# A transformer block on one Trainium2 core: modulation sums turned a block sooner, dilated attention's steps four chunks later, the first gate's rows with priority, the background's modulation begun sooner

## The chip, the core and the metric

The kernel runs on one core of one Trainium2 chip. The metric is device time in microseconds (us). The kernel before took 1590.88 us, the median of three runs (1590.88, 1587.47, 1592.99). One further execution was recorded by the hardware profiler; every row quoted is from that one.

## The reference

One decoder block on x of 256 tokens by 2048 channels, in float32, with a conditioning vector c:

```python
mod = silu(c) @ w_ada + b_ada            # 2048 x 12288
shift1, scale1, gate1, shift2, scale2, gate2 = split(mod, 6)
h = rms_norm(x, norm1_gain) * (1 + scale1) + shift1
x = x + gate1 * mixing_sublayer(h, w_in, ...)
h = rms_norm(x, norm2_gain) * (1 + scale2) + shift2
x = x + gate2 * swiglu(h, w_ffn_in, w_ffn_out)
```

The mixing sublayer projects h by w_in into the columns of three mixers (stick-breaking attention, six heads; dilated window attention, six heads in three groups; gated linear attention, four heads) and into three sigmoid gates of 2048 columns each. Each mixer's output goes through its own matrix (w_br_sb, w_br_dil, w_br_gla), is multiplied by its gate, and the sum y goes through w_out. All weights are float32 and are read once.

## The kernel before, in words

**Products.** Every float32 operand is split in two parts, `hi` (rounded) and `lo` (the rest), and a product is three matmuls, hi·hi, hi·lo and lo·hi (L171 to L173 in `mm3`). The tokens are two tiles of 128, the channels of K are 16 chunks of 128, and a block is 512 columns of output: 6 matmuls of 128x128 by 128x512 for each chunk of K. Weights come two chunks at a time, 512 KB a DMA: SyncE issues the load into `raw`, ScalarE casts it to `whi` (L163; L522 in the grouped part), VectorE subtracts to `wlo` (L164; L523). Each has four buffers. One such weight group feeds 12 matmuls. ScalarE and VectorE work through their instructions in the order given, and so does SyncE's queue.

**Order.** The program is written in one order, and a scheduler that knows priorities lays it out on each engine. `prio()` moves what stands in it ahead, `issue_after` ties an instruction behind another one.

**The start: five groups of K.** h needs the modulation of its chunk, and that needs a pass over w_ada. So the first 16 blocks of w_in are computed group by group: GROUPS cuts the 16 chunks into 2, 3, 3, 3 and 5. While the blocks of group g run, `ada_stream` loads w_ada for group g + 1, and VectorE adds it up (`ada_mac`, L298: one multiply-add of 128 rows by the width). A finished piece is turned into columns by `turn_piece`: TensorE transposes it (L366), VectorE reduces (L368), adds the bias (L374) and finishes the scale (L377). `h_group` (L553 on) then makes H for the next group: ScalarE writes the high half (L487) and a float copy (L493), VectorE the low half (L494). The last block of a group is carried into the next one. The turning happens ahead of the group's last block (n == GROUPED - 1, L663), and h_group behind that block for the first and the fourth group change, ahead of it for the two between.

**The last group and the mixers.** The 16 blocks of the last group run with steps of the mixers put between their chunks of K (`steps` of `block`, tied behind the last matmul). `qk_norm` (L699) normalises the heads of q and k on ScalarE and VectorE (L717), `qk_turn` transposes them (L729) and ScalarE copies them back with the gain (L730). For dilated attention the turns are steps 7 and 10 of the block of columns 14·512, and the scores steps 13 and 15. Its weights and the mixture's rows follow with priority, then the gate blocks, the first with no steps, the second with the mixture's products.

**The background.** The rest of the modulation (shift2, gate1, scale2: 96 loads of 512 KB of w_ada) runs beside all this: `tick` in `block` advances a generator by the current rate for each weight group. A step issues one load on SyncE's queue (L413) and, where the ring of buffers is full, the multiply-add of an earlier one (L298). The ring has two tiles (AR0, AR1) until the blocks 13 to 15 of the last group, then four. The rate is 0 in blocks 0 to 4 of the last group, RATE_IN = 0.8 from block 5, RATE_MID = 0.7 from block 13 to the end of the y blocks. When gate1 is summed, `rows_of` (L1049) turns its four quarters of 512 columns into rows on all partitions: for each half quarter a cast (L1059), a subtraction (L1060) into `T6`, and, two ticks later, two matmuls with ones (L1064, L1065).

**The y blocks.** `y_block(n)` multiplies the three mixers' outputs by 512 columns of w_br_sb, w_br_dil and w_br_gla, and by the gates (L1213 to L1216). y(0) runs around 590 us, y(1) around 660 us.

Of the kernel before, what the change touches and what calls it, by code (L numbers as in the profile page):

```python
# [10 lines left out]
F32 = mybir.dt.float32  # L11
# [3 lines left out]
ALU = mybir.AluOpType  # L15
# [14 lines left out]
N_DIL = 6  # L30
N_GLA = 4
SEG_SHIFT1, SEG_SCALE1, SEG_GATE1, SEG_SHIFT2, SEG_SCALE2, SEG_GATE2 = range(6)
RATE_IN, RATE_MID = 0.8, 0.7

RATES_OP, RATES_FFN, RATE_OUT = (0.8, 0.3, 0.0), (0.75, 0.9, 0.7, 0.6), 0.5
GATE2_CUT = 12
# [4 lines left out]
GROUPED = 16  # L41
# [37 lines left out]
def trunk(ctx: ExitStack, tc: tile.TileContext, I, out):  # L79
    nc = tc.nc  # L80
# [24 lines left out]
    def acc_bank(shape=None):  # L105
        return psa.tile(shape or [P, NB], F32, tag="acc", name=nm("acc"))
# [4 lines left out]
    @contextmanager  # L111
    def prio(offset=AHEAD):

        with tc.high_priority(offset=offset):
            start = tc.cur_priority
            yield
            n = tc.cur_priority - start
        tc.cur_priority += n

    state = {"rate": 0.0}  # L120
# [387 lines left out]
    LAST = len(GROUPS) - 1  # L508
# [44 lines left out]
    def h_group(g):  # L553
        k0, k1 = GROUPS[g]
        sh, sc = gains[g]
        for k in range(k0, k1):
            make_h(k, sh[:, k - k0 : k - k0 + 1], sc[:, k - k0 : k - k0 + 1], g == 0)
# [96 lines left out]
    for g in range(LAST):  # L654
        base = ADA_BY[g - 1] if g else 0
        for n, b in enumerate(orders[g]):
            due = ADA_BY[0] * n // (GROUPED - 2) if g == 0 else base + (ADA_BY[g] - base) * (n + 1) // (GROUPED - 2)
            while done < min(due, ADA_BY[g]) and next(nxt, "end") != "end":
                done += 1
            if (g, n) == (0, 6):  # L660
                state.pop("casts_after", None)
                state.pop("macs_after", None)
            if n == GROUPED - 1:  # L663
                while turns and (g == LAST - 1 or turns[0][0] <= ADA_LATE + KC * (g + 1)):
                    turns.pop(0)[1]()
                if 0 < g < LAST - 1:
                    h_group(g + 1)
            if n % 2 == 0:
                two = early if (g, n) == (0, 0) else load_two(b - b % 2, *GROUPS[g])
            proj_block(g, b, two[b % 2], carry=n == GROUPED - 1)  # L670
        if g in (0, LAST - 1):
            h_group(g + 1)

    kc = S("KC", [P, 8, P])
    low_r, bias = S("T3", [P, P], F32R), kc[:, 1, :]
# [45 lines left out]
    def qk_turn(parts, behind=None):  # L721

        for b, h0, h1, gain in parts:
            for h in range(h0, h1, 2):
                ps = misc_bank([P, NT, 2, P])
                for t in range(NT):
                    for i in range(2):
                        with tc.issue_after(behind) if behind is not None else nullcontext():
                            nc.tensor.transpose(ps[:, t, i, :], heads(b)[:, t, h + i, :], ident)  # L729
                nc.scalar.activation(heads(b)[:, :, h : h + 2, :], ps, AF.Copy, scale=gain(h))  # L730
# [213 lines left out]
    dil_parts = ((4, 2, 4, dil_q), (5, 0, 4, dil_q), (6, 0, 4, dil_k), (7, 0, 2, dil_k))  # L944
# [44 lines left out]
    def mixture_rows(prob, sm, lse, den, spans):  # L989
        G = lambda x, g: x[:, :, 2 * g : 2 * g + 2]  # L990
        coef = const.tile([P, NT, N_DIL], F32, name="dcoef")
        for g in range(3):
            nc.vector.tensor_mul(G(coef, g), G(sm, g), den)
        nc.vector.reciprocal(coef, coef)
        nc.vector.tensor_mul(coef, coef, lse)
        for h in range(N_DIL):
            p = prob[h // 2][:, h % 2, :]
            for t, (a, b) in enumerate(spans):
                nc.vector.tensor_scalar(p[:, a:b], p[:, a:b], coef[:, t, h : h + 1], None, op0=ALU.mult)
# [49 lines left out]
    def rows_of(name, seg, acc):  # L1049

        quarters = [a[:, c : c + NB] for a in acc for c in (0, NB)]
        for _ in range(4):
            yield
        for q in quarters:
            ps = misc_bank([P, NB])
            for c in (slice(0, T), slice(T, NB)):
                hl = S("T6", [P, 2, T], F32R)
                hi, lo = hl[:, 0, :], hl[:, 1, :]
                nc.scalar.copy(hi, q[:, c])  # L1059
                nc.vector.tensor_tensor(lo, q[:, c], hi.bitcast(F32), op=ALU.subtract)  # L1060
                yield
                yield
                with tc.issue_after(state["mm"].ins):
                    nc.tensor.matmul(ps[:, c], ones_r, hi, start=True, stop=False)  # L1064
                    nc.tensor.matmul(ps[:, c], ones_r, lo, start=False, stop=True)  # L1065
            nc.scalar.copy(q, ps)
            yield
        state[name] = quarters
# [4 lines left out]
    def background():  # L1073
        for seg in (SEG_SHIFT2, SEG_GATE1, SEG_SCALE2):
            if seg == SEG_GATE1:
                acc = biased([S(f"T{4 + j}", [P, 2 * NB]) for j in range(2)], seg)
                yield from ada_segment_steps(acc, seg, rows_of("gate1", seg, acc), False)
            else:
                acc = S("ada", [P, D])
                yield from ada_segment_steps(halves(acc), seg, columns(seg, acc))  # L1080
        yield from last_macs()

    bg.append(background())
    for b in range(0, 3):
        proj_block(LAST, b)
    qk_norm(sb_parts)
# [13 lines left out]
    for b in range(13, GROUPED):  # L1100
        proj_block(LAST, b)

    dil_scores, dil_weights = dilated()
    dil_steps = {
        7: lambda: qk_turn(dil_parts[:2], state["mm"].ins),
        10: lambda: qk_turn(dil_parts[2:], state["mm"].ins),
        13: lambda: dil_scores(0, 3),
        15: lambda: dil_scores(3, 6),
    }
    pss = [acc_bank() for _ in range(NT)]  # L1110
    block(pss, h_at, w_in, 0, KC, 14 * NB, steps=dil_steps)
    rr = [A[13], S("A1", [P, NT, NB])]
# [8 lines left out]
    def gate_block(n, br, steps=None):  # L1121
        pss = [acc_bank() for _ in range(NT)]
        c0 = COL_G + br * D + n * NB
        block(pss, h_at, w_in, 0, KC, c0, steps=steps)
        g = S(gtags[n, br], [P, NT, NB])
        with prio():
            for t in range(NT):
                if n == 0:
                    state["gates0"] = nc.scalar.copy(g[:, t, :], pss[t])
                else:  # L1130
                    nc.scalar.activation(g[:, t, :], pss[t], AF.Sigmoid)
        gates[n, br] = g

    with prio():
        groups = dil_weights()
        mixture_rows(*groups)
    gate_block(0, 0)
    ring["tags"] = ("AR0", "AR1", "KC", "KD")
    od, turns = mixture(groups[0])
    gate_block(0, 1, turns)  # L1140
# [7 lines left out]
    for j in range(2):  # L1148
# [3 lines left out]
        for t in range(NT):  # L1152
            for h in (2 * j, 2 * j + 1):
                o, c = og[t][:, h, :], t * N_GLA + h
# [4 lines left out]
    for j in range(2):  # L1159
        hi = S(gtag[0][j], [P, 4, T], F32R)  # L1160
        lo = S(gtag[1][j], [P, 4, T], F32R)
        for t in range(NT):
            o = og[t].rearrange("p h d -> p (h d)")
            ps = misc_bank([P, 4, P])
            for i in range(4):
                c = 4 * j + i
# [346 lines left out]
    for i in range(NFF):  # L1513
# [32 lines left out]
        if ftags[2 * i] == ftags[2 * i + 1]:  # L1546
            hl = S(ftags[2 * i], [P, 2, 4, T], F32R)
            hi, lo = hl[:, 0], hl[:, 1]
# [99 lines left out]
    n, pss = 3, o[1]  # L1648
# [42 lines left out]
```

## Time and profile before

| | |
|---|---|
| runs | 1590.88, 1587.47, 1592.99 us |
| profiled execution | 1591.43 us |
| its span, first to last instruction | 1589.6 us |
| mean granted TensorE clock | 0.997 |
| TensorE busy | 1570.5 us, 99% |
| VectorE busy | 1335.3 us, 84% |
| ScalarE busy | 933.3 us, 59% |
| DMA | 402.25 MB, mean 253 GB/s |

Line numbers (L171) are those of the kernel's source. PE is TensorE, PEld its weight loads, DVE VectorE, ACT ScalarE, SP SyncE. Numbers at the end of buffer names are left out in rows of the profile. A row of the timeline gives the start and the length in us, and, in brackets, the idle time of the engine before it and what ended it. Matmuls overlap: one lasts 0.39 us in the rows, the next starts about 0.23 us behind it.

### The profile page before, as it was taken

The numbers are of one execution on the slowest core, as the hardware profiler recorded it, in microseconds if no ns is written. First come the engines' busy times: TensorE is split into PE (matmuls) and PEld (weight loads), VectorE is DVE, ScalarE is ACT, GpSimd is POOL, SyncE is SP. The second block draws the span as 40 slices with busy tenths as digits, with TensorE's granted clock in tenths as the row PEclk, the third lists the DMA queues.
The fourth block names the chain that finished last, engine by engine and source line by source line (L and its number), as shares of the span: only waits on it lengthen the run. The fifth ranks groups of instructions, "written<-read, shape, count | busy, mean of one in ns | idle before, by whom it ended". The sixth has DMA issues, their size and how long they took to land.

```text
span 1589.6 us, 20243 instructions
## 1 busy us (share of the span) xinstructions
PE 1570.5 (99%) x7190; PEld 1296.6 (82%) x7190; DVE 1335.3 (84%) x1615; ACT 933.3 (59%) x1331; POOL 13.3 (1%) x24
## 2 busy tenths in 40 slices
PE   8999999999999999999999999999999999999999
PEld 7788788888878878878888888888888888888887
DVE  6878886589888878878777887999999999999996
ACT  6777777887675534444445644555555555455553
POOL 1000000000000000000000000000000000000000
PEclk9999999999999999999999999999999999999999
DMA  9989987667787899988786786665565666975664
GB/s 339 331 309 311 317 313 278 207 210 233 225 275 261 287 330 331 309 290 310 239 280 233 271 290 217 202 198 197 200 210 196 202 199 205 311 236 193 218 213 147
DMA packets 185228, 402.25 MB, mean 253 GB/s; under 512 B 13278, under 2 KB 32388, under 8 KB 185128
## 3 DMA queue, kind: packets, MB, share of 16 engines
q1 hardware_dynamic: 183864, 397.75, 74.1%
q0 software_dynamic: 1088, 3.16, 0.6%
q8 instruction: 56, 0.92, 0.2%
q14 instruction: 44, 0.36, 0.1%
q10 hardware_dynamic: 176, 0.07, 0.0%
HBM read 395.68 MB, written 5.24 MB: 252 GB/s over the span
## 4 chain that ended last, share of the span: by engine, by line
PE 86%; DMA 4%; ACT 4%; DVE 4%; issue 2%; SPq 0%; ACTq 0%; DVEq 0%
PE acc L172 21%; PE acc L173 21%; PE acc L171 21%; PE misc L172 6%; PE misc L173 6%; PE misc L171 6%; DMA raw<-w_in 2%; ACT whi L163 1%; DVE wlo L164 1%; DMA raw<-w_br_gla 1%; PE misc L883 1%; PE misc L1198 0%; ACT A L549 0%; PE misc L467 0%; DVE wlo L523 0%
## 5 line engine op out<-in xcount | busy, mean ns | idle before, releaser
L171 PE MATMUL acc<-whi,H 128*128 128x512 f32 x1145 | 448.7, 393 | 3.6 <-ACT H L487 3.3
L172 PE MATMUL acc<-wlo,H 128*128 128x512 f32 x1145 | 448.6, 392 | 1.6 <-DVE wlo L523 1.6
L173 PE MATMUL acc<-whi,H 128*128 128x512 f32 x1145 | 446.9, 391 | 0.1
L163 ACT CAST whi<-raw 128x1024 fp32r<-128x1024 f32 (+1 forms) x232 | 237.0, 1023 | 246.2 <-PE acc L173 150.6
L164 DVE TENSOR_TENSOR wlo<-raw,whi 128x1024 fp32r<-128x1024 f32 (+1 forms) x232 | 274.0, 1185 | 111.0 <-ACT whi L163 104.8
L171 PEld LDWEIGHTS acc<-whi,H 128*128 128x128 f32 x1145 | 215.9, 189 | 48.7 <-ACT H L487 3.9
L172 PEld LDWEIGHTS acc<-wlo,H 128*128 128x128 f32 x1145 | 215.9, 189 | 47.9 <-DVE wlo L523 4.4
L173 PEld LDWEIGHTS acc<-whi,H 128*128 128x128 f32 x1145 | 215.5, 188 | 45.6 <-DVE H L494 0.6
L1420 ACT CAST whi<-raw 128x1024 fp32r<-128x1024 f32 (+1 forms) x163 | 155.3, 968 | 112.4 <-PE acc L173 42.3
L1406 DVE TENSOR_TENSOR wlo<-raw,whi 128x1024 fp32r<-128x1024 f32 (+1 forms) x163 | 178.1, 1115 | 10.8 <-ACT whi L1420 9.8
L523 DVE TENSOR_TENSOR wlo<-raw,whi 128x1024 fp32r<-128x1024 f32 x86 | 103.9, 1221 | 28.3 <-ACT whi L522 27.9
L549 ACT COPY A<-acc 128x512 f32<-128x512 f32 x129 | 73.5, 585 | 44.7 <-PE acc L173 43.3
L522 ACT CAST whi<-raw 128x1024 fp32r<-128x1024 f32 x86 | 89.7, 1053 | 7.5 <-DMA raw<-w_in 4.0
L173 PE MATMUL acc<-whi,A 128*128 128x512 f32 x234 | 91.1, 389 | 0.0
L172 PE MATMUL acc<-wlo,A 128*128 128x512 f32 x224 | 87.4, 390 | 0.8 <-DVE wlo L164 0.8
L171 PE MATMUL acc<-whi,A 128*128 128x512 f32 x224 | 87.6, 391 | 0.2 <-ACT whi L163 0.2
L171 PE MATMUL misc<-whi,H 128*128 128x512 f32 (+1 forms) x201 | 78.2, 389 | 0.0
L172 PE MATMUL misc<-wlo,H 128*128 128x512 f32 (+1 forms) x201 | 78.1, 388 | 0.0
L173 PE MATMUL misc<-whi,H 128*128 128x512 f32 (+1 forms) x201 | 77.9, 388 | 0.0
L1420 ACT CAST A<-raw 128x1024 fp32r<-128x1024 f32 (+1 forms) x47 | 45.9, 989 | 33.5 <-PE acc L173 12.8
L1406 DVE TENSOR_TENSOR A<-raw,A 128x1024 fp32r<-128x1024 f32 (+2 forms) x59 | 61.2, 1049 | 4.6 <-ACT A L1420 4.2
L539 ACT COPY acc<-A 128x512 f32<-128x512 f32 x97 | 56.1, 595 | 6.9 <-DVE A L551 6.0
(511 smaller groups left out, 2605.1 us busy)
## 6 DMA issues: line engine op xcount, KB each, us to landing
raw<-w_in SPq DMA_DIRECT2D x210, 512.0 KB, 5.1
raw<-w_ffn_in SPq DMA_DIRECT2D x176, 512.0 KB, 4.6
raw<-w_ffn_out SPq DMA_DIRECT2D x74, 512.0 KB, 5.4
AR<-w_ada SPq DMA_DIRECT2D x58, 512.0 KB, 5.0
raw<-w_out SPq DMA_DIRECT2D x32, 512.0 KB, 4.9
KC<-w_ada SPq DMA_DIRECT2D x23, 512.0 KB, 5.7
KD<-w_ada SPq DMA_DIRECT2D x20, 512.0 KB, 5.5
OS<-w_ada SPq DMA_DIRECT2D x24, 384.0 KB, 6.4
```

The costliest lines, as they stand in the source:

```text
L163: state["cast"] = nc.scalar.copy(hi[:, :n, :], raw[:, :n, :])
L164: state["split"] = nc.vector.tensor_tensor(lo[:, :n, :], raw[:, :n, :], hi[:, :n, :].bitcast(F32), op=ALU.subtract)
L171: nc.tensor.matmul(ps, lh, rh, start=start, stop=False, skip_group_check=seeded)
L172: nc.tensor.matmul(ps, lh, rl, start=False, stop=False, skip_group_check=seeded)
L173: state["mm"] = nc.tensor.matmul(ps, ll, rh, start=False, stop=stop, skip_group_check=seeded)
L522: nc.scalar.copy(hi, raw)
L523: nc.vector.tensor_tensor(lo, raw, hi.bitcast(F32), op=ALU.subtract)
L539: nc.scalar.copy(pss[t], A[b][:, t, :])
L549: nc.scalar.copy(A[b][:, t, :], pss[t])
L883: nc.tensor.matmul(ps[:n, t * N_GLA + h, :].rearrange("p (s l) -> p s l", l=L), at(f, h, t)[:, :n], odd(at(f, h, t)), start=True, stop=True,)
L1406: done = nc.vector.tensor_tensor(dst, x, y, op=ALU.subtract)
L1420: nc.scalar.copy(hi[:, :n, :], src)
```

## The change

Five edits. (1) The turning of the modulation's sums, and h_group, move one block up: the turning stands ahead of block 14 of each group, h_group ahead of block 15, for every group alike. (2) The cast and the subtraction of gate1's rows get priority. (3) The dilated turns go from steps 7 and 10 of their block to 11 and 14. (4) The scores go from that block's steps 13 and 15 into steps 1 and 3 of the first gate block, and the weights and the mixture's rows behind them into the same step 3. (5) The background begins at rate 0.5 in blocks 0 to 4 of the last group, and RATE_MID falls from 0.7 to 0.62.

```diff
-RATE_IN, RATE_MID = 0.8, 0.7
+RATE_FIRST, RATE_IN, RATE_MID = 0.5, 0.8, 0.62
...
-            if n == GROUPED - 1:
+            if n == GROUPED - 2:
                 while turns and (g == LAST - 1 or turns[0][0] <= ADA_LATE + KC * (g + 1)):
                     turns.pop(0)[1]()
-                if 0 < g < LAST - 1:
-                    h_group(g + 1)
+            if n == GROUPED - 1:
+                h_group(g + 1)
             if n % 2 == 0:
                 two = early if (g, n) == (0, 0) else load_two(b - b % 2, *GROUPS[g])
             proj_block(g, b, two[b % 2], carry=n == GROUPED - 1)
-        if g in (0, LAST - 1):
-            h_group(g + 1)
...
-                nc.scalar.copy(hi, q[:, c])
-                nc.vector.tensor_tensor(lo, q[:, c], hi.bitcast(F32), op=ALU.subtract)
+                with prio():
+                    nc.scalar.copy(hi, q[:, c])
+                    nc.vector.tensor_tensor(lo, q[:, c], hi.bitcast(F32), op=ALU.subtract)
...
     bg.append(background())
+    state["rate"] = RATE_FIRST
...
     dil_steps = {
-        7: lambda: qk_turn(dil_parts[:2], state["mm"].ins),
-        10: lambda: qk_turn(dil_parts[2:], state["mm"].ins),
-        13: lambda: dil_scores(0, 3),
-        15: lambda: dil_scores(3, 6),
+        11: lambda: qk_turn(dil_parts[:2], state["mm"].ins),
+        14: lambda: qk_turn(dil_parts[2:], state["mm"].ins),
     }
+    groups = []
+
+    def dil_last():
+        dil_scores(3, 6)
+        groups.extend(dil_weights())
+        mixture_rows(*groups)
+
...
-    with prio():
-        groups = dil_weights()
-        mixture_rows(*groups)
-    gate_block(0, 0)
+    gate_block(0, 0, {1: lambda: dil_scores(0, 3), 3: dil_last})
```

**Where VectorE's instructions stand at the first group change.** `tiny` are the sums, `mod1` the columns, `AR0` the sum of the group after next, `H4` the low half of h. Before:

```order
L523 TENSOR_TENSOR wlo_163_704<-raw_161_701,whi_162_703 128x1024
L296 TENSOR_SCALAR AR0_179_771<-OS2_180_772,csil_91 128x768
L523 TENSOR_TENSOR wlo_166_710<-raw_164_707,whi_165_709 128x1024
L523 TENSOR_TENSOR wlo_183_778<-raw_181_775,whi_182_777 128x1024
L368 TENSOR_REDUCE tiny_170_730<-misc_171_731 128x3
L368 TENSOR_REDUCE tiny_172_737<-misc_173_738 128x3
L374 TENSOR_TENSOR mod1_101<-tiny_170_730,bada_100 128x3
L523 TENSOR_TENSOR wlo_186_784<-raw_184_781,whi_185_783 128x1024
L374 TENSOR_TENSOR mod1_101<-tiny_172_737,bada_100 128x3
L523 TENSOR_TENSOR wlo_189_790<-raw_187_787,whi_188_789 128x1024
L377 SCALAR_TENSOR_TENSOR mod1_101<-mod1_101,vec_99 128x3
```

The same place with the change:

```order
L523 TENSOR_TENSOR wlo_167_719<-raw_165_716,whi_166_718 128x1024
L368 TENSOR_REDUCE tiny_161_701<-misc_162_702 128x3
L368 TENSOR_REDUCE tiny_163_708<-misc_164_709 128x3
L374 TENSOR_TENSOR mod1_101<-tiny_161_701,bada_100 128x3
L523 TENSOR_TENSOR wlo_170_725<-raw_168_722,whi_169_724 128x1024
L374 TENSOR_TENSOR mod1_101<-tiny_163_708,bada_100 128x3
L296 TENSOR_SCALAR AR0_179_771<-OS2_180_772,csil_91 128x768
L377 SCALAR_TENSOR_TENSOR mod1_101<-mod1_101,vec_99 128x3
L523 TENSOR_TENSOR wlo_183_778<-raw_181_775,whi_182_777 128x1024
L523 TENSOR_TENSOR wlo_186_784<-raw_184_781,whi_185_783 128x1024
L298 SCALAR_TENSOR_TENSOR AR0_179_771<-OD_191_814,csil_91,AR0_179_771 128x768
L523 TENSOR_TENSOR wlo_189_790<-raw_187_787,whi_188_789 128x1024
```

The columns (L377) now stand ahead of the splits wlo_183, wlo_186 and wlo_189. On TensorE the six transposes go from behind block 14's last matmul to ahead of its first.

ScalarE's order there is the same before and after but for buffer numbers; with the change:

```order
L522 CAST whi_182_777<-raw_181_775 128x1024
L549 COPY A14_173_742<-acc_171_728 128x512
L549 COPY A14_173_742<-acc_172_729 128x512
L522 CAST whi_185_783<-raw_184_781 128x1024
L539 COPY acc_194_821<-A14_173_742 128x512
L522 CAST whi_188_789<-raw_187_787 128x1024
L487 ACTIVATE H0_15_112<-T0_6_102,mod1_101 128x256
```

H (L487) did not move against the copies of block 14 and the casts.

**Where VectorE's subtraction of gate1's rows stands**, at the half of the rows that is the fifth of eight. `T6` is the half's low part, `ada` the sum of scale2. Before:

```order
L164 TENSOR_TENSOR wlo_1345_6180<-raw_1343_6177,whi_1344_6179 128x1024
L1215 TENSOR_TENSOR A8_1181_5427<-A8_1181_5427,acc_1314_6067 128x512
L1215 TENSOR_TENSOR A8_1181_5427<-A8_1181_5427,acc_1315_6068 128x512
L1216 TENSOR_TENSOR T3_1291_5966<-T3_1291_5966,A8_1181_5427 128x512 x2
L164 TENSOR_TENSOR wlo_1348_6186<-raw_1346_6183,whi_1347_6185 128x1024
L298 SCALAR_TENSOR_TENSOR ada_1246_5658<-KC_1312_6044,csil_91,ada_1246_5658 128x1024
L164 TENSOR_TENSOR wlo_1351_6192<-raw_1349_6189,whi_1350_6191 128x1024
L1060 TENSOR_TENSOR T6_1332_6142<-T5_1015_4533,T6_1332_6142 128x256
```

With the change (the line is L1059 there):

```order
L164 TENSOR_TENSOR wlo_1325_6087<-raw_1323_6084,whi_1324_6086 128x1024
L164 TENSOR_TENSOR wlo_1328_6093<-raw_1326_6090,whi_1327_6092 128x1024
L1059 TENSOR_TENSOR T6_1332_6130<-T5_967_4245,T6_1332_6130 128x256
L298 SCALAR_TENSOR_TENSOR ada_1218_5554<-AR1_1306_5995,csil_91,ada_1218_5554 128x1024
L164 TENSOR_TENSOR wlo_1339_6168<-raw_1337_6165,whi_1338_6167 128x1024
```

It stands five splits earlier: wlo_1339, 1342, 1345, 1348 and 1351 now follow it. On TensorE, before, two full weight groups (those of 1345 and 1348) come between the matmuls of this half and the first that reads wlo_1351; with the change the matmuls of the half stand behind the first group of 1339.

**SyncE's queue at the first y block.** Before, from the first load of w_br_gla to the second:

```order
L149 DMA raw_1203_5521<-w_br_gla 128x2x512
L413 DMA KC_1179_5398<-w_ada 128x1024
L413 DMA KD_1180_5413<-w_ada 128x1024
L413 DMA AR0_1194_5464<-w_ada 128x1024
L413 DMA AR1_1195_5479<-w_ada 128x1024
L149 DMA raw_1206_5527<-w_br_gla 128x2x512
```

With the change:

```order
L149 DMA raw_1206_5530<-w_br_gla 128x2x512
L413 DMA KC_1183_5422<-w_ada 128x1024
L413 DMA KD_1197_5473<-w_ada 128x1024
L413 DMA AR0_1203_5510<-w_ada 128x1024
L149 DMA raw_1209_5536<-w_br_gla 128x2x512
```

One background load less stands among the block's weights.

## The prediction

> **What bounds the kernel now.** I read the head of the profile first.
>
> ```profile
> span 1589.6 us, 20243 instructions
> ## 1 busy us (share of the span) xinstructions
> PE 1570.5 (99%) x7190; PEld 1296.6 (82%) x7190; DVE 1335.3 (84%) x1615; ACT 933.3 (59%) x1331; POOL 13.3 (1%) x24
> ```
>
> From the 40 slices of the span I take what the DMAs moved.
>
> ```profile
> GB/s 339 331 309 311 317 313 278 207 210 233 225 275 261 287 330 331 309 290 310 239 280 233 271 290 217 202 198 197 200 210 196 202 199 205 311 236 193 218 213 147
> ```
>
> TensorE is busy 99% of the span, so no gain larger than its idle time, plus whatever its slow clock costs, can come from a change that leaves every matmul in place. The profiled execution took 1591.43 us, 1.83 us more than its span and 0.55 us more than the median shown, 1590.88. The sum below is made against 1591.43, and 0.55 is taken off at the end. The slices of 330 and 331 GB/s are the stretch 556 to 636 us, to which I return.
>
> Next, the waits of TensorE: engine, line, what it waited for, then us in total, times, longest.
>
> ```profile
> PE acc L171 <- ACT H L487: 3.3, 2, 3.0
> PE misc L1065 <- DVE T L1060: 2.9, 1, 2.9
> PE misc L225 <- DMA H<-c: 2.4, 1, 2.4
> PE acc L172 <- DVE wlo L523: 1.6, 2, 1.0
> PE misc L729 <- DVE A L717: 1.4, 1, 1.4
> ```
>
> The rest of the list is 1.3 us or less each. The first, second and fifth row name lines that the change touches: the group's h (L487), the rows of gate1 (L1060), the dilated step's normalisation (L717). Of the small ones, one is weights that came late where the background's loads compete with them; it is quoted below.
>
> A stall costs more than its own length if the clock falls. The table by stretch shows for each: us, busy time of TensorE, its weight loads, VectorE, ScalarE and GpSimd, the granted clock, DMA share and GB/s. I laid the stretches on the edges at which the clock changed.
>
> ```profile
> 72.70:76.13 3.43, 0.59 (x3) 0.49 (x4) 3.23 (x6) 2.06 (x4) 0.00 (x0) 1.00 0.94 329
> 76.13:79.54 3.41, 3.41 (x10) 2.64 (x9) 3.27 (x6) 2.75 (x5) 0.00 (x0) 0.50 0.94 311
> 79.54:82.95 3.41, 3.41 (x16) 2.81 (x15) 1.61 (x2) 1.12 (x3) 0.00 (x0) 1.00 1.00 372
> ```
>
> The same about the second stall:
>
> ```profile
> 676.88:680.29 3.41, 0.56 (x6) 0.32 (x3) 1.92 (x4) 2.44 (x3) 0.00 (x0) 1.00 0.99 359
> 680.29:683.70 3.41, 3.39 (x9) 2.71 (x10) 2.63 (x4) 1.02 (x3) 0.00 (x0) 0.50 0.86 273
> ```
>
> Each of the two long stalls leaves a stretch of 3.4 us with TensorE busy for only 0.6 us, and the next stretch runs at clock 0.50: 10 and 9 matmuls begin in it instead of 16. At 3.41/16 = 0.213 us apiece that is 1.3 us and 1.5 us lost. The two stalls thus cost 3.0 + 1.3 = 4.3 us and 2.9 + 1.5 = 4.4 us.
>
> **First part: modulation sums one block sooner (L663 on).** This is the first stall, between group 0 and group 1.
>
> Its rows of TensorE (start and length in us, engine, line, operation, and in brackets the idle time before it), then ScalarE's, then VectorE's:
>
> ```profile
> 70.30 0.81 PE L366 MATMUL misc<-ident,ada 128*128 128x128 f32 x6
> 70.87 0.47 PE L171 MATMUL acc<-whi,H 128*128 128x512 f32 x1
> ...
> 75.54 0.50 PE L171 MATMUL acc<-whi,H 128*128 128x512 f32 x1 [3.04 <-ACT H L487]
> ```
>
> ```profile
> 72.47 1.05 ACT L522 CAST whi<-raw 128x1024 fp32r<-128x1024 f32 x1
> 74.89 0.60 ACT L487 ACTIVATE H<-T,mod 128x256 fp32r<-128x256 f32 x1 [1.37 <-DVE mod L377]
> ```
>
> ```profile
> 74.70 0.15 DVE L377 SCALAR_TENSOR_TENSOR mod<-mod,vec 128x3 f32<-128x3 f32 x1
> ...
> 76.75 0.42 DVE L494 TENSOR_TENSOR H<-scr,H 128x256 fp32r<-128x256 f32 x1
> ```
>
> TensorE runs out of work at 75.54 − 3.04 = 72.50, and waits for H until 75.54. H waited for the last modulation column on VectorE (74.70 + 0.15 = 74.85), although ScalarE was free from 72.47 + 1.05 = 73.52 on. The change turns the sums before block 14 instead of after it, so the six transposes go some 18 matmuls, 18 × 0.226 = 4 us, earlier (40.00 us for the 177 matmuls of the row of 278 below), and the order on VectorE puts L377 ahead of two weight splits of 1.2 us that stood before it. The columns are then ready well before 73.5. What is late next is ScalarE: its order is unchanged, and two copies of block 14, a cast, a copy and another cast stand ahead of H. The transposes now run ahead of block 14, so its end moves back by about the 0.57 us that they took (70.30 to 70.87) less one matmul of 0.23 that now comes after: some 0.35 us. ScalarE is free at 73.52 + 0.35 = 73.87, and H follows it: TensorE starts 0.65 us after H starts, as before (74.89 to 75.54), at 74.5 instead of 75.54. The stall shrinks from 3.04 to about 2.0 us: −1.05. It does not vanish.
>
> The second half of the product needs the low half (L494), which ran at 76.75. In the new order it stands behind one split less on VectorE, and follows at about 76.4. From 74.5 TensorE has 8 matmuls of 0.23 us that need only H, until 76.3: 0.1 to 0.5 us of new wait, I take 0.3.
>
> Does the clock still fall? With a stall of 2.0 us that stretch is busy for about 1.6 of 3.4 us. No row shows such a share. The nearest row is at the dilated step:
>
> ```profile
> 458.42:461.83 3.41, 2.04 (x11) 1.38 (x10) 2.07 (x3) 2.22 (x3) 0.00 (x0) 1.00 1.06 405
> 461.83:465.24 3.41, 3.41 (x24) 2.81 (x23) 3.37 (x6) 2.94 (x5) 0.00 (x0) 1.00 0.89 340
> ```
>
> There 2.04 us busy left the next stretch at 1.00; 0.59 us did not. 1.6 lies nearer 2.04, so I take no loss: −1.3, with 0 as the other end. First part: −1.05 − 1.3 + 0.3 = **−2.0 us**, between +0.3 (TensorE no sooner, and the low half late) and −4.3.
>
> The Trainium skill ("TensorE: Matmul & The Clock Gate", Part 1) puts the half rate behind at least one idle window of about 3.4 us, on a free-running grid. The grid agrees with the rows; the idle window does not quite, since a window with 0.59 us busy was already enough. By the page's rule neither 3.04 nor 2.0 us within a window would cost anything beyond itself, and this part would be worth −0.75 us in place of −2.0; the row at 76.13 speaks for the second.
>
> At the later group changes h is made earlier too. TensorE has no such wait there (of the 3.3 us of the first row of waits, 3.0 is this stall), so I count nothing.
>
> **Second part: priority for the rows of gate1 (L1059, L1060).**
>
> ScalarE's row, VectorE's two, and TensorE's:
>
> ```profile
> 677.62 1.04 ACT L163 CAST whi<-raw 128x1024 fp32r<-128x1024 f32 x1 [5.46 <-DMA raw<-w_in]
> ```
>
> ```profile
> 678.70 1.23 DVE L164 TENSOR_TENSOR wlo<-raw,whi 128x1024 fp32r<-128x1024 f32 x1 [1.49 <-ACT whi L163]
> 679.84 0.42 DVE L1060 TENSOR_TENSOR T<-T,T 128x256 fp32r<-128x256 f32 x1
> ```
>
> ```profile
> 680.31 0.58 PE L1065 MATMUL misc<-T,ones_r 128*128 128x256 f32 x1 [2.88 <-DVE T L1060]
> ```
>
> The subtraction of 0.42 us stood on VectorE behind a weight split that waited for a cast, and that for a DMA. TensorE stood behind it though the weights of that DMA were not its next ones. With priority the subtraction stands ahead of this split, behind splits of weights that TensorE needs sooner than the gate's rows in any case. What is late next: the split that it overtakes ended at 678.70 + 1.23 = 679.93, and its weights come two weight groups, 2 × 12 matmuls × 0.226 = 5.4 us, after the gate's rows. From 677.4, where TensorE would go on, that is 682.8: 2.9 us in hand. That cover hides it. All eight halves of the gate's rows are ordered this way; the other seven did not wait before. So the wait and the slow stretch go: −2.9 − 1.5 = **−4.4 us**, between 0 (the wait moves to weights that come late, below) and −4.4.
>
> **Third part: the dilated steps four chunks later (L1104 on).**
>
> VectorE's rows and TensorE's:
>
> ```profile
> 459.76 1.22 DVE L164 TENSOR_TENSOR wlo<-raw,whi 128x1024 fp32r<-128x1024 f32 x1 [1.61 <-ACT whi L163]
> 460.90 2.49 DVE L717 TENSOR_TENSOR A<-A,tiny 128x512 f32<-128x512 f32 x4
> ```
>
> ```profile
> 461.64 1.04 PE L729 MATMUL misc<-ident,A 128*128 128x128 f32 x6 [1.38 <-DVE A L717]
> ```
>
> The normalisation of A5 stood on VectorE behind a split whose weights were late, and the transposes (L729) waited. In the program the steps go four chunks later; in TensorE's order they stand within the same weight group of the gate block as before, since the normalisation itself sets when they can run. On VectorE half of A5 now passes the split, the other half is still behind one, and two multiply-adds of the background, 1.28 us each by the row below, are new ahead of the whole chain.
>
> ```profile
> 453.47 1.28 DVE L298 SCALAR_TENSOR_TENSOR ada<-AR,csil,ada 128x1024 f32<-128x1024 f32 x1
> ```
>
> They may push the stall up by 2.6 us, or the split-free half may take away the 1.38. I take **0**, between −1.4 and +2.6. The scores and the mixture's rows move with the steps into the first gate block. Their consumer, the mixture's transposes at chunk 4 of the second gate block, stays 17 chunks of six matmuls, 17 × 6 × 0.226 = 23 us, behind: nothing. The 16 transposes of shift2's columns come earlier, between the same matmuls: nothing.
>
> **Fourth part: the background's rates.** RATE_FIRST starts the background in the last group's first five blocks.
>
> ```profile
> 278.00:318.00 40.00, 40.00 (x177) 32.81 (x176) 23.47 (x35) 35.85 (x97) 0.00 (x0) 1.00 0.67 206
> ```
>
> And the stretch of the y blocks:
>
> ```profile
> 598.00:638.00 40.00, 40.00 (x183) 33.22 (x182) 33.20 (x34) 18.99 (x22) 0.00 (x0) 1.00 0.93 332
> ```
>
> Five blocks of three weight groups (two chunks of K, 12 matmuls, 2.72 us) at 0.5 make 7.5 steps, each a DMA of 0.52 MB and 1.28 us on VectorE: 9.6 us on an engine busy for 23.5 of 40, and 3.9 MB in 40 us, 98 GB/s on top of 206. 304 GB/s is less than the 332 seen. Both hide it. RATE_MID from 0.7 to 0.62 takes 0.08 × 0.52 MB per weight group, 15 GB/s, off the stretch that runs at 332. There the weights of w_br_gla came late:
>
> ```profile
> 594.18 0.51 PE L171 MATMUL acc<-whi,A 128*128 128x512 f32 x1 [0.20 <-ACT whi L163]
> 595.45 0.50 PE L172 MATMUL acc<-wlo,A 128*128 128x512 f32 x1 [0.76 <-DVE wlo L164]
> ```
>
> In SyncE's order three background loads instead of four stand between the first and the second of these weights. One load less (0.52 MB at 332 GB/s, 1.6 us) covers 0.96 us of waits: **−1.0 us**, between 0 and −1.0. Against it I put **+0.5 us** for the weights of the next y block: seven background loads stand on SyncE's queue up to their last one, as before, but three of them now stand right ahead of the third, and no row there shows a wait now, and the price is between 0 and the 1.0 of its sister.
>
> **Sum.** −2.0 − 4.4 + 0 − 1.0 + 0.5 = −6.9 us: 1591.43 − 6.9 = 1584.5 on the profiled execution's basis, less 0.55: **1584.0 us**, −0.43%. If each part reaches its better end: −4.3 − 4.4 − 1.4 − 1.0 = −11.1, 1579.8.
>
> **Rivals.**
> (a) *The order of ScalarE decides, and the first part gives nothing.* H waits for casts whose DMAs also compete; the clock still falls. For it: five instructions stand ahead of H. Against: ScalarE idled 1.37 us before H. −4.4 − 1.0 + 0.5: 1590.88 − 4.9 = 1586.0. Here this part of the change does not do what it says.
> (b) *The DMA becomes the bound after 558 us.* TensorE comes 4.4 us earlier to every weight after 677, and if the queue had no slack, the wait returns at the next late weight: only the first part stays, 1590.88 − 2.0 = 1588.9. For it: 332 GB/s is the most any slice shows, and a cast waited 5.46 us for a DMA at 677. Against: the weights overtaken had 2.9 us in hand, and the stretch from 680 on already falls to 273 GB/s.
> (c) *The early background makes weights late in the last group.* Its loads stand on SyncE's one queue ahead of weights, each waits until VectorE has released one of only two buffers, and VectorE's multiply-add may itself stand behind a split. At the dilated step this mix cost 1.4 us, at the gate's rows 2.9 + 1.5 = 4.4. If three of the five blocks between 278 and 318 us pay 4.4 each, 13.2 − 6.9 = +6.3: 1597.2, slower. Two such stalls leave +1.9, no change that shows; it decides from the third on. Against: VectorE at 59% and 206 GB/s there.
>
> **How the numbers follow.** A measurement of this kernel can tell about 0.3%, 4.8 us, from no change: faster is below 1586.1, slower above 1595.7. Forecast 0.50, (a) 0.15, (b) 0.24, (c) 0.11. The forecast's own range is 1579.8 to 1586.1. (a) lies on the edge: two thirds of it count as faster. Faster 0.50 + 0.10 = 0.60, same 0.05 + 0.24 = 0.29, slower 0.11. The range takes in the forecast's best end, (a) and (b) with the 2.6 us of the dilated step on top (1588.9 + 2.6 = 1591.5), and leaves (c) out: 1579.5 to 1592.
>
> **What would show it.** Right: no wait at the gate's rows near 675 us and no stretch at clock 0.50 behind it; a wait of about 2 us for H near 74 us without a slow stretch; the wait for A5 near 460 us still there; none at w_br_gla near 590. Wrong: waits for weights (L171 or L172 on casts and splits) in the last group's blocks before 320 us, at the y blocks, or behind the gate's rows, or a new slow stretch anywhere.

## The result, and the profile after

With the change the kernel takes 1588.57 us, the median of 20 runs (1584.67 to 1593.55); before, 1591.27 us in 20 runs (1587.26 to 1594.34). The ratio is 0.9986, with a 95% interval of 0.9977 to 0.9995: faster, by 0.14%, some 2.2 us (2.7 us by the medians), where 0.43% was forecast. The forecast had called less than 0.3% no change; with twenty runs of each kernel the interval leaves 1 out. The profiled execution of the changed kernel took 1588.55 us.

The head of its profile:

```profile
span 1586.7 us, 20238 instructions
## 1 busy us (share of the span) xinstructions
PE 1566.8 (99%) x7190; PEld 1294.0 (82%) x7190; DVE 1334.0 (84%) x1615; ACT 932.2 (59%) x1331; POOL 12.5 (1%) x24
```

The span is 2.9 us shorter, and the work is the same: 7190 matmuls. The waits of TensorE, in the same columns as before, tell more:

```profile
PE misc L727 <- DVE A L715: 3.7, 3, 2.3
PE acc L172 <- DVE wlo L523: 3.6, 4, 1.5
PE misc L225 <- DMA H<-c: 2.4, 1, 2.4
PE acc L171 <- ACT H L487: 2.3, 2, 2.0
```

Against the list of before, the wait at the gate's rows (2.9 us) is gone, and the wait for H went from 3.3 to 2.3 us. But the splits L523 went from 1.6 to 3.6 us, and the normalisation (L715 now, L717 before) from 1.4 to 3.7. So 3.9 us less on two rows and 4.3 us more on two others, and what is left of the gain is mostly the two slow stretches of the clock, 1.3 + 1.5 us, which this execution doesn't have. The first of the two comes and goes from run to run, with the change and without it, as the last section shows; so this one pair of traces flatters the change.

**The first group change came out as forecast.** TensorE, then ScalarE, then VectorE:

```profile
74.08 0.50 PE L171 MATMUL acc<-whi,H 128*128 128x512 f32 x1 [2.03 <-ACT H L487]
...
76.71 0.73 PE L173 MATMUL acc<-whi,H 128*128 128x512 f32 x2 [0.52 <-DVE H L494]
```

```profile
72.48 1.05 ACT L522 CAST whi<-raw 128x1024 fp32r<-128x1024 f32 x1
73.43 0.61 ACT L487 ACTIVATE H<-T,mod 128x256 fp32r<-128x256 f32 x1
```

```profile
69.28 0.16 DVE L377 SCALAR_TENSOR_TENSOR mod<-mod,vec 128x3 f32<-128x3 f32 x1
...
76.24 0.42 DVE L494 TENSOR_TENSOR H<-scr,H 128x256 fp32r<-128x256 f32 x1
```

The columns are ready at 69.4 instead of 74.9. H follows directly on the cast, with no idle time before it: ScalarE's order has become the limit. The stall is 2.03 us (forecast 2.0), the new wait for the low half 0.52 (forecast 0.3). The stretch with the stall is busy for 1.94 us, and the next runs at full clock:

```profile
72.61:76.02 3.41, 1.94 (x8) 1.42 (x8) 3.41 (x4) 3.41 (x7) 0.00 (x0) 1.00 0.98 369
76.02:79.44 3.42, 2.90 (x13) 2.25 (x13) 3.38 (x6) 1.41 (x2) 0.00 (x0) 1.00 0.92 303
```

**The gate's rows too.** TensorE goes from the weights through the two matmuls with ones and on, with no idle time:

```profile
675.79 0.28 PE L1063 MATMUL misc<-T,ones_r 128*128 128x256 f32 x1
675.91 0.29 PE L1064 MATMUL misc<-T,ones_r 128*128 128x256 f32 x1
676.03 0.40 PE L171 MATMUL acc<-whi,H 128*128 128x512 f32 x1
```

**What came in their place, first: splits in the grouped part.** VectorE and TensorE around 192 us with the change:

```profile
191.19 0.89 DVE L298 SCALAR_TENSOR_TENSOR AR<-OS,csil,AR 128x640 f32<-128x640 f32 x1 [1.74 <-DMA OS<-w_ada]
192.43 0.89 DVE L298 SCALAR_TENSOR_TENSOR AR<-OD,csil,AR 128x640 f32<-128x640 f32 x1 [0.35 <-DMA OD<-w_ada]
193.23 2.36 DVE L523 TENSOR_TENSOR wlo<-raw,whi 128x1024 fp32r<-128x1024 f32 x2
```

```profile
194.50 0.50 PE L172 MATMUL acc<-wlo,H 128*128 128x512 f32 x1 [1.53 <-DVE wlo L523]
```

The two splits stand behind two multiply-adds, and VectorE waits for their loads. (The next waits of this row are 1.03 us at 212 us and 0.85 us at 247 us.) On SyncE's queue these loads were issued after two loads of weights:

```profile
183.56 2.03 SPq L519 DMA_DIRECT2D raw<-w_in  x2
185.63 0.43 SPq L337 DMA_DIRECT2D OS<-w_ada  x1
186.11 0.43 SPq L337 DMA_DIRECT2D OD<-w_ada  x1
```

Before, the load of OS was issued with two others ahead of those weights:

```profile
181.72 1.38 SPq L337 DMA_DIRECT2D OS<-w_ada  x3
185.87 2.03 SPq L519 DMA_DIRECT2D raw<-w_in  x2
187.94 0.43 SPq L337 DMA_DIRECT2D OD<-w_ada  x1
```

**Second: the stick-breaking turn.** VectorE's rows and TensorE's around 315 us with the change:

```profile
315.23 1.28 DVE L298 SCALAR_TENSOR_TENSOR ada<-AR,csil,ada 128x1024 f32<-128x1024 f32 x1
317.62 0.29 DVE L800 TENSOR_TENSOR T<-raw,T 128x128 fp32r<-128x128 f32 x1 [1.12 <-ACT T L799]
...
319.73 2.55 DVE L164 TENSOR_TENSOR wlo<-raw,whi 128x1024 fp32r<-128x1024 f32 x2 [0.57 <-PE acc L173]
322.20 1.29 DVE L715 TENSOR_TENSOR A<-A,tiny 128x512 f32<-128x512 f32 x2
```

```profile
322.94 0.77 PE L727 MATMUL misc<-ident,A 128*128 128x128 f32 x5 [2.31 <-DVE A L715]
```

Two of the early background's multiply-adds (the other at 313.94) and a subtraction that waited for a late load push the normalisation of A0 behind two more splits; TensorE waits 2.31 us.

### The profile page after: what moved, and what is told of

Its sections match the earlier page's. It is cut to its first block, busy times and chain, and to the rows that moved or that the text cites. A ratio compares the mean times of both kernels' runs of the same rounds, so it can differ in the third digit from the quotient of the medians.

```text
span 1586.7 us, 20238 instructions
## 1 busy us (share of the span) xinstructions
PE 1566.8 (99%) x7190; PEld 1294.0 (82%) x7190; DVE 1334.0 (84%) x1615; ACT 932.2 (59%) x1331; POOL 12.5 (1%) x24
## 3 DMA queue, kind: packets, MB, share of 16 engines
q1 hardware_dynamic: 183864, 397.75, 74.2%
## 4 chain that ended last, share of the span: by engine, by line
PE 82%; DMA 7%; DVE 5%; ACT 4%; issue 2%; SPq 0%; ACTq 0%; DVEq 0%
PE acc L173 19%; PE acc L172 19%; PE acc L171 19%; PE misc L172 6%; PE misc L173 6%; PE misc L171 6%; DMA T<-w_ada 2%; DMA raw<-w_in 2%; DMA OS<-w_ada 2%; DVE wlo L523 1%; ACT whi L163 1%; DMA A<-w_ada 1%; ACT scr L707 1%; PE misc L881 1%; DVE wlo L164 1%
## 5 line engine op out<-in xcount | busy, mean ns | idle before, releaser
L523 DVE TENSOR_TENSOR wlo<-raw,whi 128x1024 fp32r<-128x1024 f32 x86 | 104.1, 1221 | 25.8 <-ACT whi L522 25.6
```

Source lines behind the costliest of these rows:

```text
L523: nc.vector.tensor_tensor(lo, raw, hi.bitcast(F32), op=ALU.subtract)
```

## The experiments

Two theories stood against each other. **A:** the parts that were forecast gave what was forecast, and two side effects took most of it back: turning sooner reorders the loads of w_ada further on, and the early background makes the stick-breaking turn late. **B:** one shared cause, or VectorE's load in general, so that no single edit gives the time back. Ratios are to the kernel before, runs of which stood beside each.

**e1: no early background.**

```diff
-RATE_FIRST, RATE_IN, RATE_MID = 0.5, 0.8, 0.62
+RATE_FIRST, RATE_IN, RATE_MID = 0.0, 0.8, 0.62
```

> The changed kernel with rate 0 in blocks 0 to 4 of the last group, as before the change; all else changed. Theory A (the early background's multiply-adds and loads made the stick-breaking turn late): the wait of L727 for A L715 near 320 us falls from 2.3 us to under 0.5, and the time is some 2 us below the changed kernel's, ratio to before about 0.997. Theory B (that wait comes from the new modulation turns ahead of it): it stays near 2.3 us, ratio about 0.9985.

1585.92 us, ratio 0.9971 (0.9956 to 0.9985). The wait of L727 near 320 us is gone; what remains of that row, 0.5 us, lies at the dilated step. The splits stay late:

```profile
PE acc L172 <- DVE wlo L523: 3.5, 2, 1.9
...
PE misc L727 <- DVE A L715: 0.5, 1, 0.5
```

As A expected. The early background costs some 2.4 us by the ratios; their intervals overlap, and the pair e2 and e5 gives the same, 2.2 us.

**e2: old turns.** The turning and h_group as before, the rest changed:

```diff
-            if n == GROUPED - 2:
+            if n == GROUPED - 1:
                 while turns and (g == LAST - 1 or turns[0][0] <= ADA_LATE + KC * (g + 1)):
                     turns.pop(0)[1]()
-            if n == GROUPED - 1:
-                h_group(g + 1)
+                if 0 < g < LAST - 1:
+                    h_group(g + 1)
...
+        if g in (0, LAST - 1):
+            h_group(g + 1)
```

> The changed kernel with the modulation sums turned where they were before, all else changed. Theory A (turning sooner saves 2.1 us at the first group change and costs 3.0 us at later splits L523, since the loads of w_ada come later in SyncE's order): the 3.0 us wait for H near 75 us and its slow stretch are back, the waits for L523 splits fall from 3.6 us to about 1.6, net about 1 us faster than the changed kernel, ratio to before about 0.998. Theory B (the later splits were late for another cause): waits for L523 stay near 3.6 us and the time is 2 us above the changed kernel's, ratio about 1.000.

1585.61 us, ratio 0.9969 (0.9954 to 0.9984). The wait for H is back, the splits are in time:

```profile
PE acc L171 <- ACT H L487: 3.1, 1, 3.1
...
PE acc L172 <- DVE wlo L523: 0.2, 1, 0.2
```

The splits are as A expected, and the time by more: by the ratios 2.7 us below the changed kernel. The two intervals overlap, but e4 and the pair e1 and e5 show the same sign. So the edit that shortens the first stall is, as a whole, a loss. One thing that A expected did not come: behind the wait for H the clock stayed at 1.00 here. Another stall, of 1.43 us for the multiply-adds at 26 us, left two stretches at 0.50; the first of them:

```profile
23.11:26.53 3.42, 2.00 (x12) 1.41 (x10) 2.10 (x3) 0.48 (x1) 0.00 (x0) 1.00 1.03 382
26.53:29.94 3.41, 3.41 (x11) 2.63 (x11) 2.34 (x11) 2.33 (x5) 0.00 (x0) 0.50 1.02 386
```

(In this execution the wait of the stick-breaking turn was shorter, 1.3 us: the subtraction behind the late load began at 316.79 us, against 317.62 in the changed kernel.)

**e3: only the priority.** The kernel before, with `prio()` around the cast and the subtraction of gate1's rows.

> The kernel before with only the priority of the gate1 rows. Theory A (that wait and its slow stretch cost 4.4 us and nothing behind them takes the wait over): no wait at L1065, none new for weights behind 675 us, ratio 0.997. Theory B (the wait moves to weights that come late): waits on casts or splits of 2 to 4 us between 675 and 720 us, ratio 0.999 to 1.000.

1585.41 us, ratio 0.9971 (0.9958 to 0.9985): 4.6 us by the ratio (the interval allows 2.4 to 6.7). No wait at L1065 is left, and none above 0.3 us behind it, as A expected. This one edit gives twice what the whole change gives. (The profiled execution, 1583.56 us, was the fastest of the ten, and no stretch of it ran at a clock of 0.50.)

**e4: only the turns.** The kernel before, with the first edit alone.

> The kernel before with only the modulation sums turned one block sooner. Theory A: wait for H near 72 us about 2 us and no slow stretch behind it (2.1 us gained), L523 splits 3.6 us instead of 1.6 or more (3.0 us lost), ratio 1.0005. Theory B (the late splits belong to the other edits): L523 waits 1.6 us, ratio 0.9987.

1592.94 us, ratio 1.0022 (1.0007 to 1.0036). By itself the edit makes the kernel slower, by 3.5 us, which is more than A's 0.8. The wait for H is 2.0 us and the splits' 3.4, as A expected, but behind the first stall the clock fell, which A had excluded:

```profile
70.48:73.89 3.41, 1.44 (x7) 0.86 (x5) 1.92 (x2) 3.41 (x7) 0.00 (x0) 1.00 1.05 388
73.89:77.30 3.41, 3.35 (x8) 2.67 (x9) 3.41 (x5) 3.40 (x7) 0.00 (x0) 0.50 0.88 294
```

Two more slow stretches follow, behind a late split (from 248.0 us) and behind the wait at the gate's rows (from 688.3 us). Why the loss is more than 0.8 us is not settled. The profiled execution was the slowest of the twelve, 1598.60 us, and has waits that nothing here ties to the edit, 3.3 us for weights at the two y blocks, where the kernel before had 1.0.

**e5: neither turns nor early background.** Old turns and RATE_FIRST 0.0 together.

> Old turns and no early background: only the priority, the dilated steps and the rate 0.62. Theory A (sooner turns and the early background each cost 2 to 3 us, independently, and the rest keeps its gains): faster than either of the two kernels with one of them undone, 1582 us, ratio 0.995. Theory B (one shared cause, so that undoing either undoes it, and there is nothing more to gain): 1585.5 us, ratio 0.997.

1582.78 us, ratio 0.9955 (0.9939 to 0.9971), the lowest median of all, and faster than both kernels of the case. The two losses add up: undoing one gives 0.9971 or 0.9969, undoing both 0.9955. B's 0.997 lies at the edge of the interval of these five runs; what speaks against one shared cause more plainly is that each of the two waits went by itself, the turn's in e1 and the splits' in e2.

**e6: the same with the middle rate at 0.7.**

> As e5, but with the middle rate 0.7 as before: only the priority and the dilated steps. Theory A (the rate is what takes the wait for w_br_gla near 590 us away): waits on casts and splits of 0.9 us or more near 590 us are back, and the time is 1 to 1.5 us above e5. Theory B (the gain comes from where the steps of the dilated attention put the loads): no such wait, the same time as e5.

1587.73 us, ratio 0.9982 (0.9969 to 0.9995). In its rows the late weights near 594 us are back, in their share of this row:

```profile
PE acc L172 <- DVE wlo L164: 1.1, 2, 0.8
```

The longest, 0.75 us, is the one at 594; 0.40 lies at 662, the next y block. 0.9 or more had been expected at the first; by the ratios the rate is worth 0.27%, 4 us, which is more than these rows explain and more than the 1 to 1.5 expected. Its profiled execution also had two slow stretches behind the first stall (from 74.2 us on), which that of the kernel with 0.62 had not; the rate can't be their cause, since it is set only from block 13 of the last group on. Over all traces, the waits for weights at the two y blocks add up to 1.0, 1.3, 3.3 and 1.1 us at rate 0.7 (before, e3, e4, e6) and none is listed there in seven of the eight at 0.62 (0.7 us in e8). So the sign is shown, the size (1 to 4 us) is not settled.

**e7: the loads of w_ada sooner.** In the kernel of the first experiment, the load alone gets a little more priority from the 20th step on, the multiply-add keeps its own:

```diff
-                with prio():
+                with prio(AHEAD + (60 if step >= 20 else 0)):
                     raw = S(ADA_TAGS[step % len(ADA_TAGS)], [P, len(js), w])
...
+                with prio():
                     with tc.issue_after(state["macs_after"]) if "macs_after" in state else nullcontext():
                         ada_mac(acc, raw, k)
```

> The kernel with sooner turns and no early background (the first experiment), and from the 20th on the loads of w_ada of the grouped part a little sooner on SyncE's queue, ahead of the weights that they came behind. Theory A (the splits L523 are late because they stand on VectorE behind multiply-adds whose loads were issued late): the waits for L523 fall from 3.5 us to under 1.5, and the time by about 2 us, ratio 0.9955. Theory B (VectorE has too much to do there, whatever the order of loads): waits for L523 stay near 3.5 us, ratio 0.997.

1583.96 us, ratio 0.9966 (0.9953 to 0.9979). The rows are as A expected, with the turns still sooner:

```profile
PE acc L171 <- ACT H L488: 2.3, 2, 2.0
...
PE acc L172 <- DVE wlo L524: 1.1, 2, 0.6
```

The splits' wait falls from 3.5 to 1.1 us, so the late loads are the cause shown of that wait. It is no accident of one trace: with the old turns this row has 1.6, 0.8, 1.1, 0.3, 0.2 and less than 0.2 us (before, e3, e9, e6, e2, e5), with the sooner turns 3.6, 3.5, 3.4 and 4.5 (the changed kernel, e1, e4, e8). The time agrees less clearly: by the medians 2.0 us, by the ratios 0.0005, and the intervals overlap. And even so the sooner turns do not beat the old ones (e5, 0.9955).

**e8: the early background doubled.** RATE_FIRST 1.0 in the changed kernel.

> The changed kernel with the first rate 1.0 instead of 0.5, 15 loads in blocks 0 to 4 of the last group instead of 7 or 8. Theory A (its loads and multiply-adds make the stick-breaking turn late): the wait of L727 near 320 us grows from 2.3 us to 3 us or more, or weights become late before it; time 2 us or more above the changed kernel, ratio 1.000 or more. Theory B (the wait near 320 us is not from the early background): unchanged within 0.5 us, ratio 0.9986.

1596.44 us, ratio 1.0042 (1.0028 to 1.0057), 9 us above the changed kernel by the ratios. The wait did not grow at the turn, as I had expected first; it moved to the weights, between 311 and 331 us:

```profile
PE acc L172 <- DVE wlo L164: 3.4, 5, 1.2
...
PE acc L171 <- ACT whi L163: 2.2, 3, 1.0
```

And in the last group's first 40 us the DMAs moved 264 GB/s, against 260 in the changed kernel; here the doubled rate, then the changed kernel:

```profile
278.00:318.00 40.00, 38.61 (x167) 30.58 (x165) 30.71 (x39) 34.12 (x94) 0.00 (x0) 1.00 0.81 264
```

```profile
278.00:318.00 40.00, 40.00 (x177) 32.79 (x176) 28.12 (x35) 35.13 (x97) 0.00 (x0) 1.00 0.81 260
```

Eleven background loads were issued in these 40 us instead of seven, and hardly more was moved, though the share of 0.81 leaves room. A load stands on SyncE's queue until its buffer is free, and the weights stand behind it: from 278 to 332 us the background's loads waited there 16.5 us for multiply-adds to be done, against 5.2 us in the changed kernel. This is the mechanism of rival (c), at twice the dose. The waits of TensorE that the profile lists grew by 4.9 us in all, from 15.7 to 20.6, while the span grew by 7.9; where the other 3 us lie is open.

**e9: priority and rate only.** The kernel before with `prio()` at the gate's rows and RATE_MID 0.62.

> The kernel before with the priority and the middle rate 0.62, nothing else. Theory A (the dilated steps are worth nothing, the rate 1 to 2 us): as fast as e5 within 1.5 us, ratio 0.9955 to 0.996, no wait near 590 us; the wait for A5 near 455 us is there or not by up to 1.4 us. Theory B (the dilated steps gave e5 its lead over the priority alone): ratio 0.997, and a wait of 1 to 2 us near 455 us.

1584.29 us, ratio 0.9959 (0.9943 to 0.9975), within 1.5 us of e5, and its wait for A5 is 0.2 us. The dilated steps are worth nothing that can be measured, as forecast; at rate 0.7 the pair without and with them (e3, e6) gives 0.9971 and 0.9982, within the intervals too. No wait for A5 is listed in e3 either, though the engines there carry out the same instructions in the same order as in the kernel before up to 520 us. So at this place one and the same code differs by 1.4 us from run to run.

**e10: H ahead of the casts.** In the kernel of e7, `h_group` of the first group change under `prio()`.

> The kernel of e7 with h of the second group written with priority, so that ScalarE makes H ahead of the two casts and the copy that stood before it. Theory A (what is left of the first stall, 2.0 us, is ScalarE's order): the wait for H near 72 us falls under 0.5 us, the weights behind cost at most 0.7 us, and the time is 1 to 1.5 us below e7, ratio 0.9955. Theory B (H waits for the modulation columns): the wait stays near 2 us, ratio 0.9966.

1583.40 us, ratio 0.9964 (0.9953 to 0.9974): no difference from e7 that can be measured. The wait for H is gone, but the cast that H overtook is now waited for:

```profile
75.26 0.96 PE L171 MATMUL acc<-whi,H 128*128 128x512 f32 x3 [1.62 <-ACT whi L523]
```

Half a miss: ScalarE's order was what held H, and H's own work on ScalarE, six instructions of 0.6 us, then holds the weights. I had allowed 0.7 us for them; it was 1.6. (This execution, 1587.53 us, was the slowest of the twelve.) What remains at this change of groups is ScalarE's work.

## Why the prediction was right or wrong

The direction was right and the time lies in the stated range, though outside the forecast's own part of it, 1579.8 to 1586.1. The forecast's size was wrong, three times what was measured. That the time comes within 0.4 us of rival (b)'s 1588.9 is chance: (b) has the wait return at weights behind the gate's rows, and neither the changed kernel nor e3 has one there. (Its argument that 332 GB/s was the most of any slice misread the list, which has 339.) Of rival (a) one half is right, that ScalarE's order decides what is left of the first stall (e10). By the prediction's own steps:

- **Second part (gate1's rows), −4.4:** right. Alone it measured 0.9971, −4.6 us. In the two traces whose gate's rows had no priority (before, e4) a slow stretch follows that wait, and in none of the ten others is there one at this place.
- **Third part (dilated steps), 0:** right. With the steps (e5) and without them (e9) the times agree within their intervals. In the changed kernel the wait for A5 went from 1.38 to 1.22 us:

```profile
464.91 0.66 PE L727 MATMUL misc<-ident,A 128*128 128x128 f32 x4 [1.22 <-DVE A L715]
```

- **Fourth part, RATE_MID, −1.0 with +0.5 for the next y block:** right in kind. The waits at w_br_gla are gone, the next y block does not wait.
- **First part, at the first stall:** the wait was right, 2.03 us, and so was the low half, 0.52. The −1.3 for the clock ("1.6 lies nearer 2.04, so I take no loss") failed as a term: it came about in this execution by luck. A slow stretch stands behind the first stall in three of the six traces with the old turns and in three of the six with the sooner ones, as the last section shows, so no run shows that the edit saves it.
- **The other step that failed in the first part** is its last sentence: "At the later group changes h is made earlier too. TensorE has no such wait there …, so I count nothing." I priced the wait that I knew, the one for H, and not what else the moved work shifts. The order of SyncE's queue was compared only at the y block. From 180 us on it shows the loads of w_ada behind weights that they stood ahead of, and VectorE's multiply-adds stay ahead of the splits. That was 2.0 us more at L523, and as a whole the edit measured +0.22% alone where −2.0 us was forecast.
- **The step that failed in the fourth part** is "Both hide it", for the early background. VectorE at 59% and DMAs at 206 GB/s are averages over 40 us, and as averages they held (260 GB/s came where 304 was forecast); what decided was the place of two multiply-adds of 1.28 us and one late load ahead of a normalisation that TensorE waits for. It cost 2.3 us at one place. This is rival (c) in a small dose: priced as three stalls of 4.4 us or nothing, while one of 2.3 came. Doubled, it cost 9 us.

The signs of being wrong that the prediction named did not come up: it would have watched for late weights in the last group, and the time was lost at splits before that group and at a normalisation in it.

The forecast missed by 6.9 − 2.2 = 4.7 us. The two terms that failed are larger: 2.4 us for the early background, and for the turns 2.0 + 2.7 = 4.7 us between the forecast and what e2 shows them to cost within the change; together 7.1. Of the 4.7 for the turns, 2.0 are the splits and 1.3 the clock term that no run bears out; the remaining 1.4 are open. So something else gave some 2.4 us more than forecast. The rate's gain, 1 to 4 us where 0.5 net was forecast, has room for it; its size is open.

## What to carry to other kernels

When a step is moved to where its result is ready sooner, compare the order of every queue until it is the same again, not only at the step: the loss came 120 us later, by way of a scheduler that put loads behind weights. A load that issues late is paid for on the engine that stands in order behind its consumer, so a busy share of 60% is no cover at a place where one instruction holds the next. And try each edit alone: here one of five gave twice the gain of all. Last, one profiled execution is one draw: waits and slow stretches of 1 to 3 us came and went at the same place of the same code, so a term that rests on one of them needs a second trace.

## What the runs showed of the clock

I had taken the slow stretch as part of a 3 us stall. It is a matter of where the stall falls on a grid of 3.41 us, at whose edges the clock changes. (The two slow stretches of the kernel before begin at 76.13 and 680.29 us, 177 times 3.413 us apart.) The stall for H was 3.04 us in the kernel before and in the one with only the priority. In the first it lay in one stretch, busy for 0.59 us, and the next ran at 0.50. In the second it lay across two:

```profile
70.69:74.10 3.41, 1.77 (x10) 1.17 (x8) 2.97 (x6) 2.79 (x4) 0.00 (x0) 1.00 1.06 396
74.10:77.51 3.41, 2.00 (x9) 1.66 (x10) 3.38 (x6) 2.66 (x6) 0.00 (x0) 1.00 0.91 306
77.51:80.92 3.41, 3.41 (x17) 2.77 (x16) 2.87 (x5) 2.08 (x4) 0.00 (x0) 1.00 1.00 332
```

Neither was followed by a slow one. And a stall of 2.0 us (only the turns, above) left a stretch busy for 1.44 us and did halve the clock. Over all stretches of the twelve traces, laid on the grid from some 8 us to 1560 us, the share of busy time decides nearly alone. Eight had TensorE busy for 0.56 to 1.52 us (0.56, 0.59, 0.98, 1.28, 1.30, 1.44, 1.45, 1.52), and each was followed by a clock of 0.50. Of 38 with 1.58 to 2.3 us only two were. The two nearest to the edge lie in one execution, that of e1:

```profile
71.93:75.34 3.41, 1.52 (x7) 1.26 (x8) 3.41 (x4) 3.41 (x7) 0.00 (x0) 1.00 0.93 345
75.34:78.76 3.42, 3.30 (x9) 2.10 (x8) 3.42 (x6) 1.82 (x3) 0.00 (x0) 0.50 0.93 303
...
246.01:249.43 3.42, 1.58 (x6) 1.05 (x6) 3.42 (x4) 1.00 (x2) 0.00 (x0) 1.00 0.70 248
249.43:252.84 3.41, 3.34 (x15) 2.72 (x15) 1.32 (x2) 2.99 (x6) 0.00 (x0) 1.00 0.83 270
```

The two exceptions are the stretch of 2.00 us in e2 (above) and one of 1.78 us in the kernel with H ahead of the casts; why they were followed by a slow one is open. (In e2 and e6 a second slow stretch came behind the first.)

```profile
73.30:76.72 3.42, 1.78 (x8) 0.89 (x6) 2.84 (x5) 3.34 (x5) 0.00 (x0) 1.00 1.07 392
76.72:80.13 3.41, 3.41 (x8) 2.73 (x9) 3.34 (x5) 0.00 (x0) 0.00 (x0) 0.50 1.01 347
```

So a stall of 2.0 us may cost some 1.5 us on top, one of 3.04 us may cost nothing on top, and where the grid lies differs from run to run: its edge nearest to the stall lay at 76.13 us before and at 74.10 in e3. The Trainium skill ("TensorE: Matmul & The Clock Gate", Part 1) calls this window free-running, which these rows bear out; its idle window before the half rate is too strict for them, since a window busy for 1.52 us was still followed by it. For the forecast it means that the 1.3 us of the first part is a chance, and that the edit is not shown to change it. With the old turns and their stall of 3.0 us the slow stretch is there in three traces (before, e6, e9) and not in three (e2, e3, e5); with the sooner turns and a stall of 1.6 to 2.0 us it is there in three (e1, e4, e10) and not in three (the changed kernel, e7, e8).
